# Sums of down-projection weights, moved from the start of the program into the gate/up stage

## The chip, the cores and the metric

The kernel runs on one core of one Trainium2 chip. The metric is the device time of one execution in microseconds; before the change the median of three runs is 1242.08 us (1241.87 to 1243.5). Its engines are TensorE (matmuls; PE in the profile, PEld for its weight loads), VectorE (DVE), ScalarE (ACT), GpSimd (POOL) and SyncE (SP, which here issues DMAs). Each has its own queue of instructions and takes them in order. DMAs issued by SyncE go out on a queue of their own (q1), those issued by GpSimd on another (q0); both run on the same 16 DMA engines.

## The reference

An encoder trunk of two layers over x (512 x 1024, float32). Cut to what matters here:

```python
for l in range(DEPTH):                                   # DEPTH = 2
    h = rms_norm(x, pre_mix_norm[l])
    q, k, v, conv_u, gate_b, gate_c = split(h @ w_in[l])
    q, k = rotary(q, cos, sin), rotary(k, cos, sin)      # angle = position * frequency
    attn = dilated_mixture_attention(q, k, v)            # 8 heads of 64
    conv_y = gate_b * short_conv(gate_c * conv_u, conv_w[l])
    mix = concat(rms_norm(attn), rms_norm(conv_y)) @ w_out[l]
    x = x + rms_norm(mix, post_mix_norm[l])
    h = rms_norm(x, pre_ffn_norm[l])
    g, u = split(h @ w_gate_up[l])                       # 2 x 2816 columns
    x = x + rms_norm((silu(g) * u) @ w_down[l], post_ffn_norm[l])
return x
```

## The kernel before

All products run in three matmuls: each operand is split into a high part (`wh`, a rounded copy that ScalarE makes) and the rest (`wl`, which VectorE makes by subtraction), and high x high, high x low and low x high are summed. Weights come as pieces of 512 KB (128 x 1024 float32) into three buffers `raw`, by `load_raw` on SyncE; SyncE waits there until the oldest buffer is free.

Stages of a layer, in order: the values (in the first layer `first_values`, which works straight from x transposed, `big<-in_xT`, while weights and x still arrive), four pairs of q and k chunks with attention running between them, six chunks for the convolution, the output projection, the gate/up stage (22 chunks, the last 18 by a scheme of seven products, `seven`, with the weights of chunk m+1 combined by `prepare` meanwhile), and the down projection. The first sixteen row blocks of the down projection also use a scheme of seven products. It needs four sums of quarters of the weight matrix `wd`: with quarters b11, b12, b21, b22, these are t1 = b11 + b12, t3 = b12 + b22, t2 = t1 + b22, t4 = t2 + b21. They don't depend on the activations. `weight_sums` makes them by DMA alone, from device memory to device memory (`tsum`), as 16 DMAs of 1 MB per layer on GpSimd's queue; half of these add to what is there. The down projection then loads `tsum` as it loads other weights.

`weight_sums` is a generator: each `next(adding, None)` writes one DMA into the program. In before that is called in every eighth step of the q,k and convolution chunks (`advance`) and once behind each chunk of `seven`. Only TensorE and SyncE run in the order in which the code is written (`manual_schedule`). On the other engines a scheduler sets the order from what each instruction depends on. The sums depend on inputs alone, so it put all 32, of both layers, at the front of GpSimd's queue.

Also at the front of GpSimd's queue stand the rotary angles (`rotary_values`, L326 to L356): a chain of small operations on tiles of 128 x 32 that begins with the positions (`pos_sb`). ScalarE makes sine (`sn`) and cosine (`cs`) from `ang`, then changes its table of functions. `rotary_tables` clears three tiles `mid` on GpSimd (L367), fills them, and transposes them on TensorE (L382). This is called in the sixth of the eight steps of the first q,k pair, and needs also `inv`, from the squares of x that ScalarE makes as x arrives (L584).

Of the kernel before, what the change touches and what calls it, by code (L numbers as in the profile page):

```python
# [16 lines left out]
F32 = mybir.dt.float32  # L17
# [65 lines left out]
def encoder(ctx: ExitStack, tc: tile.TileContext, x, xT, pos, mask, cols, rows, w, wd, out):  # L83
    nc = tc.nc
    cpool = ctx.enter_context(tc.tile_pool(name="cpool", bufs=1))
    sb = ctx.enter_context(tc.tile_pool(name="sb", bufs=1))
# [4 lines left out]
    def nm(base):  # L91
        uid[0] += 1
        return f"{base}_{uid[0]}"

    def big(shape, dt=F32):
        return sb.tile(shape, dt, tag="big", bufs=11, name=nm("big"))
# [10 lines left out]
    def small(n, dt=F32):  # L107
        return sb.tile([P, n], dt, tag="small", bufs=24, name=nm("small"))

    def bank(tag):  # L110
        return ps.tile([P, 512], F32, tag=tag, bufs={"acc": 4, "att": 3, "pv": 1}[tag], name=nm(tag))
# [15 lines left out]
    def down_quarter(l, g, f):  # L127

        c = (2 * g + f) * KS * 512
        return wd[l][:, c:c + KS * 512]  # L130
# [15 lines left out]
    def weight_sums(l):  # L146


        b11, b12, b21, b22 = (down_quarter(l, g, f) for g in range(2) for f in range(2))
        t1, t2, t3, t4 = (tsum[l][:, k, :] for k in range(4))  # L150
        for pairs in (((t1, b11), (t3, b12)), ((t1, b12), (t3, b22)), ((t2, t1),), ((t2, b22),), ((t4, t2),), ((t4, b21),)):
            for n, (o, src) in enumerate(pairs):
                for c in range(0, KS * 512, 2048):
                    add = {"accum_op": ALU.add} if src is b22 or src is b21 or (src is b12 and o is t1) else {}
                    nc.gpsimd.dma_start(o[:, c:c + 2048], src[:, c:c + 2048], **add)
                    yield

    tc.keep_in_program_order(nc.scalar.preload_act_table_set("trig_and_small"))
# [34 lines left out]
    def warm_up():  # L193

        b = bank("att")
        for _ in range(WARM):
            nc.tensor.matmul(b[:, :P], blank, blank, start=True, stop=True)
# [35 lines left out]
    def take(n, h, keep=None):  # L233


        return take_half(2 * n + h, keep)
# [7 lines left out]
    def mm3(o, sh, sl, mh, ml, start, stop):  # L244
        nc.tensor.matmul(o, sh, mh, start=start, stop=False)  # L245
        nc.tensor.matmul(o, sh, ml, start=False, stop=False)  # L246
        nc.tensor.matmul(o, sl, mh, start=False, stop=stop)  # L247
# [31 lines left out]
    def new_hT():  # L279
        return [[big([P, 4, S], F32R) for _ in range(2)] for _ in range(2)]  # L280
# [11 lines left out]
    def transposed(t, h, hT, tag, raw=None):  # L292
        for g in range(2):
            b = bank(tag)
            for k in range(4):
                nc.tensor.transpose(b[:, k * P:(k + 1) * P], h[:, (4 * g + k) * P:(4 * g + k + 1) * P], ident)
            b4 = b.rearrange("p (k t) -> p k t", k=4)
            hi = hT[0][g][:, :, t * P:(t + 1) * P]
            lo = hT[1][g][:, :, t * P:(t + 1) * P]
            nc.scalar.copy(hi, b4)  # L300
            nc.vector.tensor_sub(lo, b4, hi.bitcast(F32))
            if raw is not None:
                nc.scalar.copy(raw[g][:, :, t * P:(t + 1) * P], b4)
# [12 lines left out]
    def pair_full(n, hT, step=None, tag="acc"):  # L316
        accs = [bank(tag), bank(tag)]
        pair_part(n, accs, hT, 0, S, step)
        return accs
# [121 lines left out]
    def run_background(n=None):  # L441

        while background and n != 0:
            try:
                next(background[0])
                n = None if n is None else n - 1
            except StopIteration:
                background.pop(0)
# [143 lines left out]
                nc.scalar.activation(V[:, t, :], accs[t], AF.Copy, scale=inv[:, 2 * t:2 * t + 1])  # L592
        return inv

    def in_proj_attention(l, hT, h, tables, adding):

        base = l * NCHUNK
        V = big([P, NT, S])
        accs = [None] * NT

        def values(t, g, turn=None):
            if accs[t] is None:
                accs[t] = bank("acc")
            for kt in range(4 * g, 4 * g + 4):
                if turn is not None and kt == 4 + TURN // 2:
                    transposed(turn, h[turn], hT, "acc")
                hi, lo = take(base + g, (kt % 4) // 2, 2 * base if t < NT - 1 else None)
                c = (kt % 2) * 512
                mm3(accs[t], hT[0][g][:, kt % 4, t * P:(t + 1) * P], hT[1][g][:, kt % 4, t * P:(t + 1) * P],
                    hi[:, c:c + 512], lo[:, c:c + 512], kt == 0, kt == KT - 1)  # L610
            if g == 1:
                nc.scalar.copy(V[:, t, :], accs[t])

        inv = None
        if l == 0:
            inv = first_values(hT, V)
            nc.sync.dma_start(mask_sb, mask)
        else:
            for o in [(0, 0), (0, 1, 2), (1, 0), (1, 1, 3), (2, 0), (2, 1), (3, 0), (3, 1)]:
                values(*o)  # L620

        qks = [None] * 4
        merged = [None] * 4
        sq_a = sb.tile([P, S], F32, tag="sqa", bufs=1, name=nm("sqa"))
        sq_c = sb.tile([P, S], F32, tag="sqc", bufs=1, name=nm("sqc"))
        att = attention(l, qks, V, merged, sq_a)
        count = [0]

        def advance():
            if count[0] % 8 == 7:  # L630
                next(adding, None)
            for _ in range(PACE[count[0] % len(PACE)]):
                next(att, None)
            run_background(BG)
            count[0] += 1

        made = []
        for j in range(4):
            if j == 1:
                merged[0:2] = [big([P, 2, 2, S], F32R) for _ in range(2)]  # L640
            seen = [0]

            def step():
                seen[0] += 1
                if l == 0 and j == 0 and seen[0] == TURN_ROT:
                    made.extend(rotary_tables(*angles, inv))
                if j > 1 or (j == 1 and seen[0] > START):
                    advance()
                elif j == 1:
                    run_background(BG)  # L650

            accs = pair_full(base + 2 + j, hT, step, "att" if l == 0 and j == 0 else "acc")
            if l == 0 and j == 0:
                tables, scaled, inv2 = made
            qk = big([P, 4, S], F32R)
            kl = sb.tile([P, 2, S], F32R, tag="kl", bufs=2, name=nm("kl"))
            background.append(rope_split(accs, scaled if l == 0 else tables, qk, kl))
            qks[j] = (qk, kl)
        merged[2:4] = [big([P, 2, 2, S], F32R) for _ in range(2)]
        kinds = ["u", "c", "b"] * 4  # L660
        held = {}
        for n in range(6):
            accs = pair_full(base + 6 + n, hT, advance)
            for m in range(2):
                i, kind = divmod(2 * n + m, 3)
                kind = "ucb"[kind]
                if kind == "u":
                    t = sb.tile([P, S], F32, tag="u", bufs=1, name=nm("u"))
                    if l == 0:
                        nc.vector.tensor_mul(t, accs[m], inv2)  # L670
                    else:
                        nc.scalar.copy(t, accs[m])
                    held["u", i] = t
                else:
                    held[kind, i] = accs[m]
                if kind == "b":
                    background.append(conv_tile(i, held["u", i], held["b", i], held["c", i], merged, l, sq_c))
        for _ in att:
            pass
        run_background()  # L680
        return merged, sq_a, sq_c, tables, inv
# [386 lines left out]
    with tc.manual_schedule(engines={mybir.EngineType.PE, mybir.EngineType.SP}):  # L1068
        warm_up()
        hs = [None] * NT  # L1070
        hT = new_hT()
        tables = None
        for l in range(DEPTH):
            adding = weight_sums(l)
            merged, sq_a, sq_c, tables, inv = in_proj_attention(l, hT, hs, tables, adding)
            hT, hs, raw = out_proj(l, merged, sq_a, sq_c, inv)
            hT, hs = feed_forward(l, hT, hs, raw, adding)

# [87 lines left out]
```

## Time and profile before

| | |
|---|---|
| median of 3 runs | 1242.08 us (1241.87 to 1243.5) |
| the profiled execution, and its span | 1242.51 us, 1240.7 us |
| busy: TensorE, VectorE, ScalarE, GpSimd | 1149.5, 848.3, 671.6, 59.5 us |
| mean granted clock of TensorE | 0.969 |
| sums from weights, `tsum<-in_wd` | 24 DMAs of 1024 KB, 12.4 us median from issue to landing |
| sums from sums, `tsum<-tsum` | 8 DMAs of 1024 KB, 9.0 us |
| weight loads `raw<-in_w` | 144 of 512 KB, 3.7 us; 8 of 256 KB, 7.9 us |
| x and x transposed | 4 of 512 KB, 30.9 us; 8 of 256 KB, 8.0 us |

All rows but the first are of one profiled execution. The page cuts the span into 40 slices of 31 us and gives each engine's busy share as a digit. A row of a timeline has the start and the length in us, the engine, the line of the code, the operation, what it writes and reads, and in brackets how long the engine stood idle before it and what ended that. A row of the waits has the total, the count and the longest. A row of a stretch has busy time of PE, PEld, DVE, ACT and POOL, each with its count, then the granted clock, the mean busy share of the DMA engines, and GB/s. "DMA to landing" is the time from issue to landing of a group of DMAs.

### The profile page before, as it was taken

To read this page: it belongs to the slowest core of one execution; us is meant where nothing else is said; L and a number is where in the kernel's file an instruction comes from. 1 tells how busy PE (TensorE), PEld (TensorE's weight loads), DVE (VectorE), ACT (ScalarE), POOL (GpSimd) and SP (SyncE) were. 2 spreads that over 40 slices of the span, in tenths; PEclk is the share of its full clock that TensorE was granted. 3 is DMA by queue.
4 is the path that set the end of the run, shared out by engine and by line. 5 is a ranking of instruction groups with operands and counts; after the bars stand their busy time and mean duration, and the time that the engine had idled before them with its cause. 6 is when DMAs were issued, how large, how long until landed. Compare 5 with 4: busy or idle time off the path is not lost.

```text
span 1240.7 us, 18112 instructions
## 1 busy us (share of the span) xinstructions
PE 1149.5 (93%) x7008; PEld 1011.3 (82%) x7008; DVE 848.3 (68%) x1392; ACT 671.6 (54%) x1263; POOL 59.5 (5%) x95
## 2 busy tenths in 40 slices
PE   8402999999999999999998999999999999999997
PEld 7302777788999999998886777778899999998886
DVE  3101897556778888889647698654876788879844
ACT  4202676535645555668444577543754656667632
POOL 4121100110000000000000000011000000000000
PEclk9755999999999999999999999999999999999999
DMA  9999942242223333356631311244212333336651
GB/s 329 291 270 263 287 118 85 69 137 85 69 79 105 106 102 103 103 170 185 206 119 52 119 66 54 68 119 119 69 55 99 103 103 103 103 107 201 200 155 69
DMA packets 41847, 162.64 MB, mean 131 GB/s; under 512 B 4896, under 2 KB 4896, under 8 KB 37664
## 3 DMA queue, kind: packets, MB, share of 16 engines
q1 hardware_dynamic: 35280, 122.64, 31.0%
q0 software_dynamic: 5760, 37.75, 11.8%
q8 instruction: 55, 0.90, 0.3%
q10 hardware_dynamic: 720, 1.09, 0.2%
q14 instruction: 32, 0.26, 0.1%
HBM read 159.36 MB, written 35.65 MB: 157 GB/s over the span
## 4 chain that ended last, share of the span: by engine, by line
PE 84%; DMA 8%; DVE 3%; ACT 2%; issue 1%; POOL 0%; SPq 0%; DVEq 0%; ACTq 0%
PE acc L897 17%; PE att L897 13%; PE acc L991 9%; PE acc L245 8%; PE acc L246 8%; PE acc L247 8%; PE att L991 4%; DMA tsum<-in_wd 3%; DMA x<-in_x 3%; PE acc L1053 3%; PE pv L482 3%; PE att L475 2%; PE att L245 2%; PE att L247 2%; PE att L246 2%; PE att L458 1%
## 5 line engine op out<-in xcount | busy, mean ns | idle before, releaser
L217 DVE TENSOR_TENSOR wl<-raw,wh 128x1024 fp32r<-128x1024 f32 x140 | 171.3, 1223 | 102.5 <-ACT wh L216 101.5
L897 PE MATMUL acc<-big,wh 128*128 128x256 f32 x1152 | 212.0, 283 | 0.0
L216 ACT CAST wh<-raw 128x1024 fp32r<-128x1024 f32 x140 | 147.3, 1053 | 112.4 <-PE acc L246 36.2
L897 PEld LDWEIGHTS acc<-big,wh 128*128 128x128 f32 x1152 | 179.8, 192 | 0.2
L897 PE MATMUL acc<-big,wl 128*128 128x256 f32 x576 | 163.0, 283 | 0.0
L897 PE MATMUL att<-big,wh 128*128 128x256 f32 x864 | 160.4, 283 | 0.0
L245 PE MATMUL acc<-big,wh 128*128 128x512 f32 (+1 forms) x400 | 154.0, 385 | 0.0
L247 PE MATMUL acc<-big,wl 128*128 128x512 f32 (+1 forms) x400 | 149.6, 374 | 0.0
L246 PE MATMUL acc<-big,wh 128*128 128x512 f32 (+1 forms) x400 | 149.3, 373 | 0.0
L897 PEld LDWEIGHTS att<-big,wh 128*128 128x128 f32 x864 | 134.7, 192 | 0.1
L897 PE MATMUL att<-big,wl 128*128 128x256 f32 x432 | 122.2, 283 | 0.0
L818 DVE TENSOR_TENSOR wl<-t,wh 128x1024 fp32r<-128x1024 f32 x72 | 88.0, 1222 | 42.7 <-ACT wh L817 42.7
L817 ACT CAST wh<-t 128x512 fp32r<-128x512 f32 x144 | 88.9, 620 | 45.8 <-PE att L897 31.7
L897 PEld LDWEIGHTS acc<-big,wl 128*128 128x128 f32 x576 | 110.6, 192 | 0.0
L991 PE MATMUL acc<-wh,big 128*128 128x512 f32 x320 | 99.5, 389 | 0.0
L817 ACT CAST wh<-raw 128x512 fp32r<-128x512 f32 x108 | 63.6, 621 | 46.1 <-PE acc L897 31.2
L247 PEld LDWEIGHTS acc<-big,wl 128*128 128x128 f32 x400 | 75.3, 188 | 13.9
L245 PEld LDWEIGHTS acc<-big,wh 128*128 128x128 f32 x400 | 75.4, 189 | 12.4 <-issue 0.8
L246 PEld LDWEIGHTS acc<-big,wh 128*128 128x128 f32 x400 | 75.6, 189 | 11.6
L818 DVE TENSOR_TENSOR wl<-raw,wh 128x512 fp32r<-128x512 f32 x72 | 68.8, 956 | 21.5 <-ACT wh L817 21.4
L897 PEld LDWEIGHTS att<-big,wl 128*128 128x128 f32 x432 | 82.9, 192 | 0.0
L991 PEld LDWEIGHTS acc<-wh,big 128*128 128x128 f32 x320 | 60.1, 188 | 12.4
(264 smaller groups left out, 2226.1 us busy)
## 6 DMA issues: line engine op xcount, KB each, us to landing
raw<-in_w SPq DMA_DIRECT2D x144, 512.0 KB, 3.7
tsum<-in_wd POOLq DMA_DIRECT2D x24, 1024.0 KB, 12.4
raw<-in_wd SPq DMA_DIRECT2D x36, 512.0 KB, 3.6
raw<-tsum SPq DMA_DIRECT2D x32, 512.0 KB, 3.7
tsum<-tsum POOLq DMA_DIRECT2D x8, 1024.0 KB, 9.0
gain<-in_rows SPq DMA_DIRECT2D x7, 512.0 KB, 5.4
big<-in_xT SPq DMA_DIRECT2D x8, 256.0 KB, 8.0
raw<-in_w SPq DMA_DIRECT2D x8, 256.0 KB, 7.9
```

What stands on the lines that cost most here:

```text
L216: nc.scalar.copy(hi, raws[i])
L217: nc.vector.tensor_sub(lo, raws[i], hi.bitcast(F32))
L245: nc.tensor.matmul(o, sh, mh, start=start, stop=False)
L246: nc.tensor.matmul(o, sh, ml, start=False, stop=False)
L247: nc.tensor.matmul(o, sl, mh, start=False, stop=stop)
L475: nc.tensor.transpose(tp[:, k * P:(k + 1) * P], sm[:, k * P:(k + 1) * P], ident)
L482: nc.tensor.matmul(o[hd * 64:hd * 64 + 64, half * 256:half * 256 + 256], V[:, k, hc:hc + 64], PT[hd][:, k, :], start=k == 0, stop=k == NT - 1)
L817: nc.scalar.copy(hi[:, c:c + 512], src[:, c:c + 512])
L818: nc.vector.tensor_sub(lo[:, :n], src[:, :n], hi[:, :n].bitcast(F32))
L897: nc.tensor.matmul(o[:, :HS], sh[:, c], mh[:, k, :], start=start and k == 0 and n == 0, stop=k == 3 and n == 2, skip_group_check=True)
L991: nc.tensor.matmul(outs[i], sh[:, k, st], mh[:, c:c + 512], start=start and k == 0 and n == 0, stop=False, skip_group_check=True)
L1053: nc.tensor.matmul(accs[f][t], sh[:, t * P:(t + 1) * P], mh[:, c:c + 512], start=False, stop=m == MT - 1 and n == 2, skip_group_check=True)
```

## The change

The calls in `advance` go; `in_proj_attention` no longer gets `adding`. What is left is one `next(adding, None)` behind each chunk of `seven`, 16 sums in 18 chunks. In front of each sum stand a fetch of one number from device memory by SyncE, whose queue is in written order, and a copy of that number by GpSimd; copy and sum are told to keep their order.

```diff
                     add = {"accum_op": ALU.add} if src is b22 or src is b21 or (src is b12 and o is t1) else {}
-                    nc.gpsimd.dma_start(o[:, c:c + 2048], src[:, c:c + 2048], **add)
+                    due = small(1)[:1]
+                    seen = sb.tile([1, 1], F32, tag="seen", bufs=2, name=nm("seen"))
+                    nc.sync.dma_start(due, cols[0:1, 0, 0:1])
+                    tc.keep_in_program_order(nc.gpsimd.tensor_copy(seen, due))
+                    tc.keep_in_program_order(nc.gpsimd.dma_start(o[:, c:c + 2048], src[:, c:c + 2048], **add))
                     yield
...
-    def in_proj_attention(l, hT, h, tables, adding):
+    def in_proj_attention(l, hT, h, tables):
...
         def advance():
-            if count[0] % 8 == 7:
-                next(adding, None)
...
-            merged, sq_a, sq_c, tables, inv = in_proj_attention(l, hT, hs, tables, adding)
+            merged, sq_a, sq_c, tables, inv = in_proj_attention(l, hT, hs, tables)
```

Lines below `weight_sums` have numbers higher by 5 in the changed kernel. GpSimd's queue before, in the middle of the angle chain (`tsum_66` holds the sums of the first layer, L155 is the sum's DMA, L342 and L343 are steps of the angles):

```order
L155 DMA tsum_66<-tsum_66 128x2048
L342 TENSOR_SCALAR small_166<-small_164 128x32
L367 MEMSET mid_416 128x512
L343 TENSOR_TENSOR ang<-ang,small_166 128x32
L367 MEMSET mid_429 128x512
L342 TENSOR_SCALAR small_166<-small_165 128x32
L367 MEMSET mid_442 128x512
L343 TENSOR_TENSOR ang<-ang,small_166 128x32
L155 DMA tsum_66<-tsum_66 128x2048
L342 TENSOR_SCALAR small_166<-small_164 128x32
L155 DMA tsum_66<-in_wd 128x2048
L343 TENSOR_TENSOR ang<-ang,small_166 128x32
```

The same queue in the changed kernel, from the last steps of the angles on (L442 belongs to the attention, L233 to the output projection):

```order
L352 TENSOR_SCALAR small_166<-small_164 128x32
L353 TENSOR_TENSOR ang<-ang,small_166 128x32
L356 TENSOR_SCALAR ang<-ang 128x32
L372 MEMSET mid_416 128x512
L372 MEMSET mid_429 128x512
L372 MEMSET mid_442 128x512
L361 TENSOR_SCALAR ang<-ang 128x32
L442 TENSOR_TENSOR sqa_364<-sqa_364,tmp_1171 128x512
L233 DMA wk_1979<-in_w 128x1024
```

No sum stands among the angles any more, and the memsets, which stood in the middle of the chain, stand behind all but its last step. Further on, in the gate/up stage of the first layer, GpSimd's queue now holds:

```order
L159 COPY seen_2956<-small_2955 1x1
L160 DMA tsum_66<-in_wd 128x2048
L159 COPY seen_3088<-small_3087 1x1
L160 DMA tsum_66<-in_wd 128x2048
L159 COPY seen_3220<-small_3219 1x1
```

where nothing stood before. SyncE's queue at the same place, where only the rows of L122 stood before (L122 is `load_raw`):

```order
L158 DMA small_2955<-in_cols 1x1
L122 DMA raw_2980<-in_w 128x1024
L122 DMA raw_3002<-in_w 128x1024
L158 DMA small_3087<-in_cols 1x1
L122 DMA raw_3112<-in_w 128x1024
L122 DMA raw_3134<-in_w 128x1024
```

Each fetch stands behind the two weight loads of a chunk. Nothing else moved on SyncE, and nothing on TensorE. On ScalarE at the start, before:

```order
L584 ACTIVATE mid_322,small_144<-x_73 128x1024
L584 ACTIVATE mid_324,small_144<-x_74 128x1024
L216 CAST wh_370<-raw_294 128x1024
L216 CAST wh_400<-raw_316 128x1024
L216 CAST wh_479<-raw_368 128x1024
L354 ACTIVATE sn<-ang 128x32
L357 ACTIVATE cs<-ang 128x32
L276 ACT_TABLE_LOAD
L263 ACTIVATE small_335<-small_144,eps_sb 128x4
```

and in the changed kernel:

```order
L589 ACTIVATE mid_322,small_144<-x_73 128x1024
L589 ACTIVATE mid_324,small_144<-x_74 128x1024
L359 ACTIVATE sn<-ang 128x32
L362 ACTIVATE cs<-ang 128x32
L281 ACT_TABLE_LOAD
L268 ACTIVATE small_335<-small_144,eps_sb 128x4
L221 CAST wh_370<-raw_294 128x1024
L270 ACTIVATE small_335<-small_335 128x4
```

The casts of weights for the second q,k pair moved behind the sine and the cosine; VectorE's subtractions that belong to them moved likewise.

## The prediction

> **What bounds the kernel now.** I read the page first, then who waited for whom, then TensorE, GpSimd and ScalarE in order of time over the first 125 us, then DMA and stretches of time.
>
> ```profile
> span 1240.7 us, 18112 instructions
> PE   8402999999999999999998999999999999999997
> PEclk9755999999999999999999999999999999999999
> DMA  9999942242223333356631311244212333336651
> ```
>
> A slice is 31 us. TensorE is full from the fifth slice on; the hole is in slices 2 to 4, where DMA is full and the clock is down. Who waited:
>
> ```profile
> PE att L382 <- DVE small L264: 60.7, 1, 60.7
> PE att L245 <- ACT wh L216: 10.3, 1, 10.3
> ACT sn L354 <- POOL ang L351: 45.3, 1, 45.3
> POOL tsum L155 <- DMA tsum<-in_wd: 56.2, 14, 9.2
> POOL tsum L155 <- DMA tsum<-tsum: 33.2, 7, 12.9
> ```
>
> TensorE's only long wait is 60.7 us at L382, the transposes of the rotary tables. Behind it ScalarE waits 45.3 us for the angle `ang` of GpSimd, and GpSimd waits 89.4 us in all for DMAs of the sums to land. GpSimd in order of time, and the last square of x on ScalarE:
>
> ```profile
> 11.36 0.66 POOL L326 CAST small<-pos_sb 128x4 f32<-128x4 int32 x1 [8.90 <-DMA pos_sb<-in_pos]
> 58.49 0.52 POOL L367 MEMSET mid<- 128x512 f32 x1 [3.20 <-ACT mid L584]
> 65.62 0.83 POOL L155 DMA_DIRECT2D tsum<-in_wd  x1 [4.32 <-DMA tsum<-tsum]
> 66.53 0.29 POOL L342 TENSOR_SCALAR small<-small 128x32 f32<-128x32 f32 x1
> 108.40 0.47 POOL L351 TENSOR_SCALAR ang<-ang 128x32 f32<-128x32 f32 x1
> 57.28 1.06 ACT L584 ACTIVATE mid<-x 128x1024 f32<-128x1024 f32 x1 [2.95 <-DMA x<-in_x]
> ```
>
> The angle chain starts at 11.36 and ends at 108.87 because a sum stands between any two of its instructions, and a sum that adds waits for an earlier one. TensorE over the same time:
>
> ```profile
> 6.29 0.51 PE L245 MATMUL acc<-wh,big 128*128 128x512 f32 x1
> 11.78 0.49 PE L245 MATMUL acc<-wh,big 128*128 128x512 f32 x1 [1.95 <-ACT wh L579]
> 22.07 0.39 PE L247 MATMUL acc<-wh,big 128*128 128x512 f32 x1
> 32.95 0.39 PE L247 MATMUL acc<-wh,big 128*128 128x512 f32 x1
> 33.17 0.39 PE L245 MATMUL att<-big,wh 128*128 128x512 f32 x1
> 49.10 0.79 PE L245 MATMUL att<-big,wh 128*128 128x512 f32 x1 [10.33 <-ACT wh L216]
> 54.20 0.40 PE L247 MATMUL att<-big,wl 128*128 128x512 f32 x1
> 115.27 1.09 PE L382 MATMUL att<-ident,mid 128*128 128x128 f32 x4 [60.67 <-DVE small L264]
> 118.50 0.63 PE L245 MATMUL att<-big,wh 128*128 128x512 f32 x1
> 121.48 0.39 PE L245 MATMUL acc<-big,wh 128*128 128x512 f32 x1
> ```
>
> The first values (96 matmuls) run from 6.29 to 33.17; the first q,k pair (48 matmuls, `att`) reaches its second half at 49.10, stops behind its sixth step, makes the transposes at 115.27, and ends at 121.48. Between 22.07 and 32.95 lie 48 matmuls: 0.2267 us each at full clock.
>
> **The change, part by part.**
>
> *Sums leave the start.* Without them GpSimd holds only the angles and three memsets there. What the angles cost by themselves:
>
> ```profile
> L329 POOL TENSOR_SCALAR ang<-col_sb,small 128x8 f32<-128x8 f32 x4 | 4.1, 1026 | 0.1
> L343 POOL TENSOR_TENSOR ang<-ang,small 128x32 f32<-128x32 f32 x6 | 2.5, 421 | 0.0
> L342 POOL TENSOR_SCALAR small<-small 128x32 f32<-128x32 f32 x6 | 1.8, 294 | 0.4
> ```
>
> These 16 take 8.4 us; the other fifteen of the chain, at about 0.4 us, some 6: 15 us. Even if the positions land no earlier than now, the angles are there at 11.4 + 15 = 26 us, not 109.
>
> What is late next is x, whose squares give `inv` and free the three tiles that GpSimd clears (the memset at 58.49 waited for the square at 57.28). Over the first 31 us the queues held:
>
> ```profile
> q1 hardware_dynamic: 2782, 5.45, 48.8%
> q0 software_dynamic: 638, 4.70, 41.8%
> ```
>
> SyncE's queue moved 5.45 MB in 48.8% of 31 us, 2.8 us of all 16 engines per MB. Up to the last piece of x it has 7.3 MB to move (16 pieces of 256 KB and 6 of 512 KB): 20 us, and with 1 us to the first issue and 2 to 3 for landing x is there at about 24 to 26 us instead of 57. Then the square (1.1), memset (0.5), the angle's last step, the cosine, the table load, `inv` and the scaled table follow. From 108.40 to the first transposes at 115.27 this tail took 6.9 us, so the transposes are ready at about 33.
>
> TensorE needs them later: if its values start at 6.3 and run through, they end at 6.3 + 96 x 0.2267 = 28.1, and the sixth step of the pair (36 matmuls) ends at 36.2. So both waits go, with 3 us to spare. In after's order ScalarE casts the later weight halves behind the sine; those serve the second pair, not this one. The terms:
> - the wait for the tables: 60.7
> - the wait for the second weight half (its cast stood behind squares that waited for x): 10.3
> - slow matmuls behind that hole: from 49.10 to 54.20 are 11 spacings, 5.1 us against 2.5: 2.6
> - transposes behind the long hole: 115.27 to 118.50 is 3.2 us in a stretch of low clock; I take 1.9 with the clock up, an estimate: 1.3
> - the first values: 26.9 us now against 21.8 run through, since the second step's data came late (1.95 us at 11.78) and the clock then fell. Between 0 and 5.1; I take 4, as the cause is the same crowded DMA.
>
> Together 78.9. Against it 1.5 us for a short wait still left at the tables (0 to 3: DMA may run a little slower than worked out). Behind it, until the sums of before are done:
>
> ```profile
> 124.00:186.00 62.00, 59.73 (x307) 47.01 (x306) 56.03 (x125) 45.03 (x84) 4.42 (x6) 1.00 0.74 203
> ```
>
> TensorE misses 2.3 of these 62 us, and VectorE has 56.0 to do in them. Weight loads get faster here, but at most 2.3 us is to be had; I count nothing.
>
> *Sums arrive in the gate/up stage.* Each of 32 sums now brings a tiny fetch on SyncE (0.33 us, like other issues there), a copy on GpSimd (at most 0.7, like the cast at L326), and the issue of the sum, 0.5 to 0.9 us. Behind the waiting copy on GpSimd stand only later sums; the next layer's `sqa` additions come after sixteen sums, which end two chunks before the stage does. What the stage has:
>
> ```profile
> 350.00:540.00 190.00, 190.00 (x1541) 188.03 (x1540) 148.26 (x199) 108.49 (x232) 0.00 (x0) 1.00 0.33 104
> 431.08 0.33 SPq L122 DMA_DIRECT2D raw<-in_w  x1
> 438.07 0.33 SPq L122 DMA_DIRECT2D raw<-in_w  x1
> 441.15 0.33 SPq L122 DMA_DIRECT2D raw<-in_w  x1
> 444.15 0.69 DVE L834 TENSOR_TENSOR t<-raw 128x512 f32<-128x512 f32 x1
> 444.95 0.69 DVE L835 TENSOR_TENSOR t<-raw,t 128x512 f32<-128x512 f32 x1
> DMA to landing us min/median/max: 3.4/3.6/4.2
> DMA to landing us min/median/max: 4.9/9.0/9.8
> q0 software_dynamic: 170, 1.26, 101.4%
> ```
>
> The first row gives busy PE, PEld, DVE, ACT, POOL: TensorE 190.00 of 190, GpSimd 0.00, VectorE 148.26, DMA share 0.33. A chunk takes 10.1 us (431.08 to 441.15, the same load of two chunks). The two landing rows are the weight loads `raw`: in this stage (3.4/3.6/4.2), and from 124 to 165 us, where sums were in flight (4.9/9.0/9.8). The last row is the sums' queue from 157 to 163 us, with adding sums alone: 1.26 MB in all of 6 us, so 5.0 us per sum of 1.05 MB, the dearest kind.
>
> Load per chunk: 0.33 x 10.1 + 5.0 = 8.3 us of 10.1. It fits. Its place: the fetch goes out right behind the load of 441.15 and lands about with it, near 445; copy, issue and first bytes bring the sum to 447 to 452. The next two loads are issued at 448.2 and 451.2. The first is wanted only 6.1 us after issue (438.07 to 444.15), 2.4 more than it needs. The second is wanted as it lands (441.15 + 3.7 against 444.95), so a tail of the sum pushed to 453 or 454 makes it about 1 us late. VectorE is idle (190.00 - 148.26)/190 x 10.1 = 2.2 us per chunk and catches that up. The cost lies between 0 and the case of the first rival; I take 1.0 us in all, near 0, because the place in the chunk keeps sum and load mostly apart.
>
> The Trainium skill, "DMA: Bandwidth & Descriptors", section "Queues, rings and completion order", says that each DMA engine takes turns between its queues packet by packet, which speaks against so mild a meeting: a load that meets a sum waits through the whole of it. By it such a load lands after 3.7 + 5.0 = 8.7 us, and the 9.0 measured from 124 to 165 us agrees; the sum would then be the first rival's, wherever they do meet.
>
> Sum: 78.9 - 1.5 - 1.0 = 76.4. The profiled execution took 1242.51 us (1.8 outside its span): 1166.1. The median of the runs, 1242.08, stands 0.4 below it: 1165.7, so 1166.
>
> **The rivals.**
> 1. *Weight loads meet the adding sums.* A load late by 5.3 us (9.0 against 3.7) less VectorE's 2.2 leaves 3.1 us per chunk in which TensorE stands. There are 8 adding sums in a layer, so 16 x 3.1 = 50 us: 1216; a part of it gives 1180 to 1216. For it: the zero slack at 444.95. Against: the load at 441.15 is issued before its own sum by construction, and the sum before has 10 us to drain.
> 2. *The same, so hard that the kernel gets slower.* All 32 chunks would stand. From 76.4/32 = 2.4 us per chunk on it decides. With loads at the longest, 9.8: 6.1 - 2.2 = 3.9 x 32 = 125 us, 1290. Against: plain sums take less of DMA than adding ones, and 8.3 of 10.1 is not full.
> 3. *x stays the brake.* If x came no earlier than 57, the transposes would start at about 64, 51 us sooner: 1191. It decides once x lands later than about 28 us. For it: x did come last, on a full DMA. Against: the software queue had 41.8% of it.
> 4. *The sums still go early*, and nothing changes: 1242. After's GpSimd order has the first one behind all work of the first attention, so it can hardly be.
>
> **How the numbers follow.** The forecast as worked out: 0.80, its own range 1157 (all 5.1 us of the first values, nothing left at the tables, and some 3 us more behind 124 us) to 1175 (a wait of 3 us left, no gain in the first values, and some 3 us lost in the gate/up stages). Rival 1: 0.09. Rival 2: 0.03. Rival 3: 0.07. Rival 4: 0.01. A measurement of this kernel can tell about 0.2%, 2.5 us, from no change. Faster holds the forecast and rivals 1 and 3: 0.96; same 0.01; slower 0.03. The range reaches from 1157 to 1192, to take in rival 3 and a light form of rival 1.
>
> **What would show it.** In the profile after: no wait of TensorE over 5 us in the first 125; `ang` done before 30 us; x landed by 28; the second pair's first `acc` matmul near 42 instead of 121.48; clock at 9 from the first or second slice on; DMA low from about 30 us on. In the gate/up stages a DMA share of 0.6 to 0.8 instead of 0.33, `raw` landing in 4 to 6 us, L835 waiting longer for it, and TensorE still busy 190 of 190. I am wrong if TensorE shows gaps in those stages or if the squares of x still end near 58.

## The result, and the profile after

The changed kernel takes 1169.97 us (median of 4 runs, 1168.72 to 1170.49), before beside it 1242.79 us: a ratio of 0.9407, 95% interval 0.9386 to 0.9428. The forecast was 1166, range 1157 to 1192. The page of the profiled execution (1170.38 us):

```profile
span 1168.4 us, 18250 instructions
PE   9999999999999999999999999999999999999997
PEclk9999999999999999999999999999999999999999
DMA  8221234222677777665223212441136776676641
```

The hole in TensorE's row is gone, and so is the low clock. DMA falls to 2 in the second slice and stands at 6 to 7 in the two stages where the sums are now. TensorE's longest waits, from who waited for whom:

```profile
PE acc L301 <- DVE small L273: 3.6, 2, 2.1
PE acc L900 <- DVE wl L821: 2.8, 4, 1.0
```

No wait is longer than 2.1 us; the second row, in the gate/up stage, is new. The start in order of time, on GpSimd, ScalarE and TensorE (L331 and L356 are the first and the next to last step of the angles, L589 the last square of x, L387 the transposes; L250 at 41.18 is the first matmul of the second pair):

```profile
7.34 0.37 POOL L331 CAST small<-pos_sb 128x4 f32<-128x4 int32 x1 [6.00 <-DMA pos_sb<-in_pos]
24.87 0.21 POOL L356 TENSOR_SCALAR ang<-ang 128x32 f32<-128x32 f32 x1
24.37 1.05 ACT L589 ACTIVATE mid<-x 128x1024 f32<-128x1024 f32 x1
36.66 0.60 PE L387 MATMUL att<-ident,mid 128*128 128x128 f32 x4
41.18 0.39 PE L250 MATMUL acc<-big,wh 128*128 128x512 f32 x1
```

The angles take 17.7 us instead of 97.5, the last square of x comes at 24.4 instead of 57.3, and the second q,k pair starts at 41.18 instead of 121.48: 80.3 us won. Then one group of matmuls of the gate/up stage, high x high into `acc`; the two times in a row are the starts of its first and its last matmul. (Lines behind `advance` stand 3 lines higher in the changed kernel, not 5: L897 is now L900, and L834 and L835 are now L837 and L838.) Before, both layers:

```profile
L897 PE MATMUL acc<-big,wh x576: 277/283/283, 366.4 to 546.3; 128*128 128x256 f32 x192
L897 PE MATMUL acc<-big,wh x576: 278/283/283, 942.4 to 1122.3; 128*128 128x256 f32 x192
```

The changed kernel:

```profile
L900 PE MATMUL acc<-big,wh x576: 278/283/285, 285.0 to 467.0; 128*128 128x256 f32 x192
L900 PE MATMUL acc<-big,wh x576: 277/283/284, 864.9 to 1049.9; 128*128 128x256 f32 x192
```

Until the first layer's gate/up stage 366.4 - 285.0 = 81.4 us are won. The stage takes 182.0 and 185.0 us instead of 179.9 twice: 7.2 us lost by this group, 7.4 from the very first to the very last matmul of the stages, the figure that the expectations below use. Between the two stages lie 397.9 us instead of 396.1: 1.8 lost. 81.4 - 7.2 - 1.8 = 72.4, and the spans differ by 72.3.

### The profile page after: what moved, and what is told of

It reads as the page before. It is cut to its first block, busy times and chain, and to the rows that moved or that the text cites. A ratio compares the mean times of both kernels' runs of the same rounds, so it can differ in the third digit from the quotient of the medians.

```text
span 1168.4 us, 18250 instructions
## 1 busy us (share of the span) xinstructions
PE 1148.5 (98%) x7008; PEld 1010.5 (86%) x7008; DVE 841.4 (72%) x1392; ACT 669.8 (57%) x1263; POOL 70.0 (6%) x127
## 4 chain that ended last, share of the span: by engine, by line
PE 44%; DVE 3%; DMA 2%; ACT 1%; issue 1%; DVEq 0%; ACTq 0%; SPq 0%
PE acc L900 7%; PE att L900 6%; PE acc L250 5%; PE acc L251 5%; PE acc L252 5%; PE acc L994 5%; PE att L994 2%; DMA raw<-in_w 2%; PE acc L1056 1%; PE pv L487 1%; PE att L480 1%; PE att L1056 1%; PE att L250 1%; PE att L252 1%; PE att L251 1%
## 5 line engine op out<-in xcount | busy, mean ns | idle before, releaser
L900 PE MATMUL acc<-big,wh 128*128 128x256 f32 x1152 | 212.2, 283 | 0.0
L900 PEld LDWEIGHTS acc<-big,wh 128*128 128x128 f32 x1152 | 179.8, 192 | 0.2
L900 PE MATMUL acc<-big,wl 128*128 128x256 f32 x576 | 163.7, 284 | 2.8 <-DVE wl L821 2.8
L900 PE MATMUL att<-big,wh 128*128 128x256 f32 x864 | 160.7, 283 | 0.2 <-ACT att L908 0.2
L250 PE MATMUL acc<-big,wh 128*128 128x512 f32 (+1 forms) x400 | 154.0, 385 | 0.0
L900 PEld LDWEIGHTS att<-big,wh 128*128 128x128 f32 x864 | 134.6, 192 | 0.5 <-ACT att L908 0.4
L900 PE MATMUL att<-big,wl 128*128 128x256 f32 x432 | 123.2, 285 | 0.4
L900 PEld LDWEIGHTS acc<-big,wl 128*128 128x128 f32 x576 | 110.5, 192 | 3.9 <-DVE wl L821 3.7
L250 PEld LDWEIGHTS acc<-big,wh 128*128 128x128 f32 x400 | 75.4, 189 | 12.3 <-issue 0.8
L900 PEld LDWEIGHTS att<-big,wl 128*128 128x128 f32 x432 | 82.8, 192 | 2.2 <-DVE wl L821 2.2
```

The source lines that it names most:

```text
L900: nc.tensor.matmul(o[:, :HS], sh[:, c], mh[:, k, :], start=start and k == 0 and n == 0, stop=k == 3 and n == 2, skip_group_check=True)
```

## The experiments

The theory after the result: the start gained because GpSimd's angle chain no longer stands between waiting sums and x no longer arrives on a crowded DMA; a part was lost again in the gate/up stage, where transfers of sums meet weight loads.

**The start: the chain alone, and the crowd alone.** To before, the sums cut short, so that they hold GpSimd but hardly move anything:

```diff
-                    nc.gpsimd.dma_start(o[:, c:c + 2048], src[:, c:c + 2048], **add)
+                    nc.gpsimd.dma_start(o[:, c:c + 64], src[:, c:c + 64], **add)
```

> The kernel before, with each of its 32 sum DMAs cut from 2048 columns to 64 (32 KB instead of 1 MB), still early on GpSimd among the angles and still waiting for one another; the down projection reads other quarters of the weights in place of the sums, so values are not the reference's. This takes GpSimd's held-up chain without the crowded DMA. Theory: some 28 issues of 0.6 us and ten waits of about 2 us stand in the 15 us chain, so the angles end at 50 to 60 us instead of 109 (and 25 without sums), TensorE stops there with its first values done at 28 and waits some 20 to 27 us: 1180 to 1190. Rival: it was the crowd alone that made the start late, and short DMAs among the angles cost nothing; then the transposes stand at 37 and the time is 1161 to 1165.

Measured: 1182.58 us (ratio to before 0.9507, 0.9491 to 0.9523). GpSimd and TensorE:

```profile
48.09 0.22 POOL L356 TENSOR_SCALAR ang<-ang 128x32 f32<-128x32 f32 x1
49.18 1.08 PE L382 MATMUL att<-ident,mid 128*128 128x128 f32 x4 [12.57 <-DVE small L264]
57.97 1.12 PE L382 MATMUL att<-ident,mid 128*128 128x128 f32 x4 [6.85 <-ACT rot L388]
```

The step of the angles that ended at 108.87 in before (L351) ends at 41.5 here, earlier than the 50 to 60 that were expected, and the last step (L356) ends at 48.3. TensorE waits 19.4 us at the transposes, though the last square of x began at 25.1 and the first values ran through. Against 1160.97 us without any sum (below) the held-up chain costs 21.6 us, even with short DMAs. To the changed kernel, nine copies whose data nobody needs:

```diff
+    spare = dpool.tile([P, 9, 2048], F32, tag="spare", name="spare")
+    for k in range(9):
+        nc.gpsimd.dma_start(spare[:, k, :], wd[0][:, k * 2048:k * 2048 + 2048])
```

> The changed kernel, and in front of everything on GpSimd nine plain copies of 1 MB from the down weights into spare device memory (9.4 MB, as much as the sums' queue moved in the first 62 us of before); none waits for another, so GpSimd's angle chain isn't held up. Nothing of the computation is left out. This takes the crowded DMA of before's start by itself. Theory: the crowd makes x late, to 40 to 50 us, and the table transposes wait for inv until some 50 to 57 us; 1170 + 10 to 20 = 1180 to 1190; the rest of the 80 us that the start won was GpSimd's chain. Rival 1: the crowd does nothing, 1170 to 1173, and the chain was all of it. Rival 2: the crowd was nearly all of it; then 1220 or more.

Measured: 1194.46 us (0.9602, 0.9589 to 0.9615), 24.5 more than the changed kernel, and 4 above the range expected.

```profile
29.99 0.21 POOL L359 TENSOR_SCALAR ang<-ang 128x32 f32<-128x32 f32 x1
PE acc L253 <- ACT wh L587: 14.3, 5, 5.1
53.80 1.05 ACT L592 ACTIVATE mid<-x 128x1024 f32<-128x1024 f32 x1
63.05 0.66 PE L390 MATMUL att<-ident,mid 128*128 128x128 f32 x4 [0.24 <-ACT rot L396]
q0 software_dynamic: 1074, 7.90, 69.8%
```

The angles are ready at 30, but the first values wait 14.3 us for weights, which was not expected, x is late (last square at 53.8), and the last group of transposes, shown here, comes 25 us later than in the changed kernel (37.94 there). The ninth copy did wait 5.1 us for an earlier one, until 10.66, but the positions landed only at 18.9, so that held no angle up. The last row is the sums' queue in the first 31 us: 7.90 MB, where before had 4.70, so this crowd is harsher than before's. Both halves of the theory hold, and each alone costs over 20 us. The two do not add up to the 80 us. That each made the other worse in before, where full transfers keep GpSimd waiting longer for a sum to land, is argued and not shown.

**The gate/up stage: what of a sum costs.** The sum DMAs left out, fetches and copies kept:

```diff
-                    tc.keep_in_program_order(nc.gpsimd.dma_start(o[:, c:c + 2048], src[:, c:c + 2048], **add))
```

> The changed kernel without the 32 sum DMAs; fetches and copies stay, and the down projection loads other quarters of the weights in place of the sums, so its values are not the reference's. Theory: the sums' transfers cost 7.4 us in the gate/up stages (their matmul streams take 183.6 and 186.6 us there against 181.4 in before). So 1162.5, and both streams 181.4. Rival: the fetches on SyncE and the copies on GpSimd cost it, then 1170 and streams as in the changed kernel.

Measured: 1160.97 us (0.9338, 0.9323 to 0.9353). Fetches and copies by themselves cost nothing; the transfers cost it. The stretches of the two gate/up stages (busy PE, PEld, DVE, ACT, POOL, then clock, DMA share, GB/s), first without sums, then in the changed kernel:

```profile
280.00:470.00 190.00, 190.00 (x1550) 188.44 (x1549) 151.60 (x201) 113.39 (x241) 5.67 (x16) 1.00 0.34 108
860.00:1045.00 185.00, 185.00 (x1529) 184.34 (x1528) 149.13 (x199) 112.65 (x239) 4.77 (x16) 1.00 0.33 107
```

```profile
280.00:470.00 190.00, 189.38 (x1541) 187.05 (x1540) 145.89 (x199) 111.92 (x239) 14.26 (x32) 1.00 0.68 191
860.00:1045.00 185.00, 182.19 (x1480) 179.36 (x1479) 137.60 (x189) 105.55 (x230) 15.09 (x32) 1.00 0.68 190
```

Next, plain copies in place of the adding ones:

```diff
-nc.gpsimd.dma_start(o[:, c:c + 2048], src[:, c:c + 2048], **add)
+nc.gpsimd.dma_start(o[:, c:c + 2048], src[:, c:c + 2048])
```

> The changed kernel with plain copies in place of the 16 adding DMAs (values are not the reference's). Theory of the prediction: adding DMAs, at 5.0 us of all DMA engines against about 2.7 to 3.5 for plain ones, are what reaches into the next load; without them the loss of 7.4 us falls to 1 or 2, so 1164. Rival: any 1 MB transfer at that place in the chunk meets the first weight load of the next chunk, since it starts 4 us before it; then the loss stays above 4 us and the time is 1167 or more.

Measured: 1162.81 us (0.9351, 0.9337 to 0.9365). Who waited for weight loads, first in the changed kernel, then here, and the matmul group of the second layer here:

```profile
DVE t L837 <- DMA raw<-in_w: 34.4, 19, 3.6
DVE t L838 <- DMA raw<-in_w: 32.4, 33, 2.1
```

```profile
DVE t L838 <- DMA raw<-in_w: 16.5, 23, 1.9
L900 PE MATMUL acc<-big,wh x576: 277/283/284, 862.5 to 1042.3; 128*128 128x256 f32 x192
```

The wait for a chunk's first load (L837; before had none at L834, and 6.3 us in all at L835) is gone again, and the stage takes 179.8 us, as without sums (179.9 and 179.8). So 32 plain transfers are hidden in full, and it is the adding ones that cost. In the changed kernel they come in a run of four and two runs of two per layer. The issues of a chunk's first load on SyncE around the run of four in the second layer:

```profile
906.43 0.33 SPq L122 DMA_DIRECT2D raw<-in_w  x1
916.37 0.33 SPq L122 DMA_DIRECT2D raw<-in_w  x1
927.83 0.33 SPq L122 DMA_DIRECT2D raw<-in_w  x1
939.48 0.33 SPq L122 DMA_DIRECT2D raw<-in_w  x1
949.14 0.33 SPq L122 DMA_DIRECT2D raw<-in_w  x1
960.83 0.38 PE L900 MATMUL acc<-big,wl 128*128 128x256 f32 x1 [0.55 <-DVE wl L821]
```

The next such issue stands at 960.80. So three of the four rounds behind 916.37 take 11.5, 11.7 and 11.7 us instead of 10.1, one takes 9.7, and TensorE stops at 960. The two longer stops of this layer, 0.88 us at 1003.77 and 0.96 us at 1035.51, stand behind the runs of two. How such a meeting looks: the adding sum issued at 913.82 moves its first data at about 915.4, and from 916.4 to 919.4 the sums' queue moves 0.64 MB and SyncE's queue nothing, although a load was issued at 916.37. VectorE gets that load at 923.94, 7.6 us after its issue. If runs are the trouble, order alone should mend it:

```diff
-        for pairs in (((t1, b11), (t3, b12)), ((t1, b12), (t3, b22)), ((t2, t1),), ((t2, b22),), ((t4, t2),), ((t4, b21),)):
-            for n, (o, src) in enumerate(pairs):
-                for c in range(0, KS * 512, 2048):
+        for pairs in (((t1, b11), (t1, b12)), ((t3, b12), (t3, b22)), ((t2, t1), (t2, b22)), ((t4, t2), (t4, b21))):
+            for c in range(0, KS * 512, 2048):
+                for n, (o, src) in enumerate(pairs):
```

> The changed kernel with its 16 sums per layer in another order: each adding DMA directly behind the plain one that it adds to, so no two adding ones follow each other. Nothing of the computation is left out. Theory: one adding sum lengthens a chunk's round of loads by some 1.4 us (load issues 11.5 us apart where adding sums 4 to 7 run), VectorE's 2.2 us catch that up in the next chunk, and only runs of two to four adding sums use up what TensorE has in front of it; alternating, the loss of 7.4 us falls to 0 to 2: 1162 to 1165. Rival: each adding sum costs its share (16 of them, 0.46 us each) wherever it stands; then 1170 as before.

Measured: 1161.27 us (0.9340, 0.9327 to 0.9352).

```profile
280.00:470.00 190.00, 190.00 (x1550) 188.47 (x1550) 149.94 (x202) 113.38 (x241) 14.46 (x32) 1.00 0.67 196
860.00:1045.00 185.00, 185.00 (x1528) 184.31 (x1528) 147.97 (x199) 112.66 (x239) 15.83 (x32) 1.00 0.66 198
DVE t L837 <- DMA raw<-in_w: 5.6, 7, 1.7
```

The same bytes and the same number of adding sums, a DMA share as high, and TensorE is full in both stretches. The median stands 0.3 us from that without sums, within the spread of either. This is the version that beats both kernels. The loss is gone as expected, but the account behind the expectation holds only in part. In the second layer the rounds in which an adding sum runs take 9.8 to 10.6 us here, against 9.7 to 12.0 in the changed kernel (the first six). So a single adding sum does not lengthen its round by 1.4 us each time, and there is less to catch up. Each adding sum is also issued further ahead of the chunk's first load, by 2.8 to 3.6 us against 1.9 to 3.2. Order is shown to decide; whether by this distance or by the run itself was not tried.

**Other places for the sums.** All 32 at once behind the angles:

```diff
+            seen = sb.tile([1, 1], F32, tag="seen", bufs=2, name=nm("seen"))
+            tc.keep_in_program_order(nc.gpsimd.tensor_copy(seen, angles[0][0:1, 0, 0:1]))
+            for g in all_sums:
+                for _ in g:
+                    pass
```

> All 32 sums go out at once again, without fetches, but behind the last step of the angles on GpSimd (a copy that waits for the cosine holds them). Nothing of the computation is left out. Theory: in before the cost was that GpSimd's angle chain stood between waiting sums, and that x came late; a full DMA behind that, from about 27 us on, costs about 1 us, and the gate/up stages get their 7.4 us back. So 1170 - 7.4 + 1 = about 1163.5, the second q,k pair starts at about 41 us as in the changed kernel, and both gate/up streams take 181.4 us. Rival: a full DMA is itself harmful, since weight loads that land after 9 us instead of 3.7 stall the attention stage; then the time is 1170 or more, and TensorE shows gaps between 40 and 170 us.

Measured: 1189.44 us (0.9564, 0.9550 to 0.9578); neither theory had it. It is one wait:

```profile
171.82 0.83 POOL L156 DMA_DIRECT2D tsum<-in_wd  x1 [4.55 <-DMA tsum<-tsum]
172.38 1.55 POOL L439 TENSOR_TENSOR sqa<-sqa,tmp 128x512 f32<-128x512 f32 x1
173.97 2.10 DVE L527 TENSOR_SCALAR tmp<-tmp,col_sb 128x512 f32<-128x512 f32 x1 [26.11 <-POOL sqa L439]
179.23 3.25 PE L484 MATMUL pv<-mid,big 128*64 128x256 f32 x13 [26.76 <-ACT mid L478]
```

The sums keep GpSimd until 172; an addition of squares stands behind the last of them and holds a buffer (`tmp`) that VectorE waits for, and with it ScalarE and TensorE. Half as many there, and the second layer's behind the first output projection:

```diff
+            for _ in all_sums[0]:
+                pass
...
             hT, hs, raw = out_proj(l, merged, sq_a, sq_c, inv)
+            for _ in all_sums[1]:
+                pass
```

> The first layer's 16 sums go out at once behind the angles (as in e1, but only half as many), the second layer's at once behind the first layer's output projection; no fetches. Nothing of the computation is left out. Theory: e1 lost 26.8 us in a single wait, because 32 sums held GpSimd until some 176 us and an addition of squares stood behind them, not because DMA was full. Sixteen sums are done at about 100 us, before that addition is due at about 109, so the wait goes: 1160 to 1163. Rival: weight loads that land after 10 us in the full stretch stall TensorE by themselves; then 1168 or more.

Measured: 1169.66 us (0.9398, 0.9385 to 0.9411): the rival's number, and its mechanism in one of the two places. The stretches from 27 to 100 us and from 200 to 285, here and in the changed kernel:

```profile
27.00:100.00 73.00, 71.45 (x362) 56.79 (x361) 61.61 (x140) 50.72 (x92) 11.25 (x17) 1.00 0.99 285
200.00:285.00 85.00, 78.87 (x491) 71.67 (x490) 60.21 (x111) 44.73 (x92) 7.08 (x10) 0.96 0.83 229
246.56 1.04 ACT L217 CAST wh<-raw 128x1024 fp32r<-128x1024 f32 x1 [7.97 <-DMA raw<-in_w]
```

```profile
27.00:100.00 73.00, 71.56 (x363) 56.89 (x362) 61.48 (x140) 50.72 (x92) 0.00 (x0) 1.00 0.24 77
200.00:285.00 85.00, 84.31 (x528) 75.80 (x527) 63.06 (x115) 46.94 (x96) 0.00 (x0) 1.00 0.26 81
```

In the attention stage a DMA share of 0.99 instead of 0.24 costs TensorE 0.1 us of 73, though the weight loads land there only after 8.3 to 16.7 us. The second batch costs 5.4 us of 85, and the clock falls with it: behind the output projection ScalarE waits 8.0 us for one weight load. Two more placements miss as well. Without fetches, only in written order:

```diff
-                    due = small(1)[:1]
-                    seen = sb.tile([1, 1], F32, tag="seen", bufs=2, name=nm("seen"))
-                    nc.sync.dma_start(due, cols[0:1, 0, 0:1])
-                    tc.keep_in_program_order(nc.gpsimd.tensor_copy(seen, due))
```

> The changed kernel without fetches and copies; the sums keep only their written order on GpSimd, so a layer's 16 sums run one after the other behind the output projection's GpSimd work, through the first gate/up chunks. Nothing of the computation is left out. Theory: the seven-product chunks are the only place where an adding sum hurts, and most sums are done before these begin, so nearly all of the 7.4 us comes back: 1161 to 1164, both streams below 182. Rival: sums in a row fill DMA, and weight loads and the splits by DMA of the output projection come late: 1167 or more.

Measured: 1176.02 us (0.9452, 0.9439 to 0.9464); the rival holds.

```profile
PE acc L246 <- ACT big L304: 9.6, 2, 5.2
```

Each layer's sums run in a row from the output projection on, and TensorE waits 9.6 us there, once in each layer. The gate/up stages are full, as expected. So the fetch, which looks like mere overhead, earns its place here. And held, but in the attention and convolution chunks:

```diff
         def advance():
+            if count[0] % 4 == 3:
+                next(adding, None)
```

> The same held sums, one behind each fourth step of the q,k and convolution chunks instead of one behind each gate/up chunk. Nothing of the computation is left out. Theory: the loads of the attention stage have room for a sum beside them, those of the gate/up stage have not. So 1163, streams of the gate/up stages 181.4 both. Rival: a sum costs as much wherever it meets weight loads; then 1168 to 1172, with gaps of TensorE in the attention and convolution stages.

Measured: 1168.34 us (0.9395, 0.9378 to 0.9412): the rival's time. The gate/up stages are full again (as expected), but 3.0 us are lost ahead of the first gate/up stage and 4.3 between the two. Of these 1.7 are a window at half clock like the one described below; the rest goes in waits of TensorE under 1 us each between convolution and output projection. The first link of a cause stands in the trace. GpSimd also issues weight loads of the output projection (L233), and the second of them in a layer now stands behind sums. Two rows of this run, then one of the changed kernel:

```profile
178.43 0.91 POOL L233 DMA_DIRECT2D big<-in_w  x1
ACT big L234 <- DMA big<-in_w: 11.5, 1, 11.5
167.94 0.59 POOL L233 DMA_DIRECT2D big<-in_w  x1
```

The load goes out 10.5 us later, and ScalarE waits 11.5 us for it; it waits as long in the second layer. How that reaches TensorE was not followed further.

## Why the prediction was right, and where not

- *The start.* Forecast 77.4 us (78.9 less 1.5), measured 80.3 at the second pair. The two waits of 60.7 and 10.3 us went in full. x landed in time as worked out from the queue's engine time, the wait left at the tables is 0.24 us instead of 1.5, and the first values gave 4.6 us instead of 4. The angles came at 25.1 against a forecast of 26, partly by luck: the chain took 17.7 us and not 15, but the positions landed 4 us earlier than in before. The tail of 6.9 us was too dear, since 5.3 of it were a wait of ScalarE for the angle's last step, which is 1.2 now; TensorE reached the transposes last, so it did not matter. The first two experiments show both causes at work.
- *The work behind 124 us.* I counted nothing; 81.4 were won by the gate/up stage, so 1.1 of the 2.3 us that could be had.
- *The sums in the gate/up stage.* This term was mis-sized: 1.0 forecast, 7.4 measured, and TensorE showed the gaps in those stages that I had named as a sign of being wrong. The load of a chunk, 8.3 us of 10.1, does fit: plain sums and alternating sums are hidden in full. What failed is the meeting of sum and load, which I took chunk by chunk and put at about 1 us, caught up by VectorE within the chunk. The load issued at 916.37 reached VectorE 7.6 us after its issue, where a load lands after 3.7 without a sum. A load that a sum makes late also delays VectorE, which frees the buffer for the next load (around the run of four all of SyncE's waits ahead of a load are for VectorE), so lateness is handed on. Three of the four rounds there were late by 1.4, 1.6 and 1.6 us, together well above VectorE's 2.2, and after two to four adding sums in a row TensorE stopped. The place was about right: I had put the sum's traffic 1.2 us ahead of the chunk's first load, and it began 1 us ahead (915.4 against 916.37).
- *The rivals.* The first had the mechanism (adding sums meet loads), with a price of 50 us that took every load as late as in the full stretch; a seventh of it came. The Trainium skill, "DMA: Bandwidth & Descriptors", section "Queues, rings and completion order", says that each DMA engine takes turns between its queues packet by packet; that a load waits through the whole of a sum was my reading of it. The trace bears that reading out in part: the load issued at 916.37 moved nothing for 3 us beside an adding sum, though it came after 7.6 us and not 8.7. Beside plain sums some loads land late too (L838 waits 16.5 us in all), yet none so late that TensorE sees it. The third (x stays the brake) did not happen; with nine copies in front it does.
- *Not foreseen:* 1.8 us between the layers. They fit one window at half clock: from 590.3 to 593.5 the granted clock is 0.50, behind it 1.00. Four matmuls in a row at its end:

```profile
593.20 0.61 PE L252 MATMUL acc<-wh,big 128*128 128x512 f32 x1
593.63 0.43 PE L250 MATMUL acc<-wh,big 128*128 128x512 f32 x1
593.89 0.40 PE L251 MATMUL acc<-wl,big 128*128 128x512 f32 x1
594.13 0.40 PE L252 MATMUL acc<-wh,big 128*128 128x512 f32 x1
```

Until 593.6 a matmul starts 0.43 us behind the one before, then 0.23 to 0.26. The profiles of before, without sums and with alternating sums have no such window there; that with plain copies has one, though its stages are full like theirs. So it does not hang on the loss in the gate/up stage. Executions of one kernel differ by as much: with alternating sums three of five took 1161.1 to 1161.3 us at a mean granted clock of 0.999, two took 1162.5 and 1162.8 at 0.998. I take the window for the way in which short waits at the layer's end fall; that was not tried.

## What to carry to other kernels

An asynchronous transfer that depends on nothing can still cost time through the queue that issues it: look at what stands behind each waiting issue, on that engine, and not only at the transfer. When background DMA goes into a full stage, check each chunk's round and then the sum over neighbouring chunks, since lateness that is handed from load to load adds up; spreading the dear transfers (every second chunk instead of two or four in a row) can hide what the mean load already allows. Before moving transfers to a quiet place, look for loads there that are wanted as they land (in the changed kernel ScalarE already waits 0.7 us for the load that waited 8.0 above): a full DMA cost 0.1 us of 73 in one stage and 5.4 of 85 in another.

## What the runs showed of the hardware

The same megabyte from device memory to device memory lands after 4.9 to 5.6 us as a plain copy in the gate/up stage, and after up to 9.2 us where half of the transfers add:

```profile
DMA to landing us min/median/max: 4.9/5.1/5.6
DMA to landing us min/median/max: 4.9/6.9/9.2
```

The first row is of the run with plain copies alone, the second of the changed kernel. I had priced the adding ones by their engine time, but not expected that they alone make the difference between hidden and not. With alternating order they land after up to 9.6 us and cost nothing that shows.
